# One layer of a hybrid decoder on one core: probabilities times values as float32 products

## The chip, the core and the metric

The kernel runs on one of the eight cores of a Trainium2 chip. A core has five engines that run side by side and wait for each other by semaphores: TensorE (PE in the profile; its weight loads are listed apart as PEld), VectorE (DVE), ScalarE (ACT), GpSimd (POOL) and SyncE (SP), which here issues the DMAs. The metric is the device time of one execution in microseconds (us).

## What is computed

One step of a decoder layer for a prompt of 1024 tokens and for 8 x 8 sampled tokens: RMS norm, an input projection to queries, keys, values and a state-space input, dilated sliding-window attention with 8 heads of 64 beside a state-space group, an output projection, and a gated feed-forward part. The change lies in the prompt's attention. For each of three branches (window, dilation) the reference computes

```python
scores = einsum('brcqhe,brckhe->brchqk', qs, kk) * HEAD_DIM ** -0.5
scores = where(mask, scores, -inf)
m = max(scores); p = exp(scores - m); den = sum(p)
out = einsum('brchqk,brckhe->brcqhe', p / den, vv)
```

and mixes the branches by their log sums. The kernel folds the three branches into two parts (`part` 0: neighbouring tokens, `part` 1: every fourth token) with scaled probabilities P, so that the output is the sum of P times V over both parts.

## The kernel before

Most large products are done in three: each float32 operand is cut into a high part, rounded to the fast type float32r (fp32r), and a low part, the remainder (`split`, lines 63 to 65: ACT writes the high part, DVE the low). `mm3` (line 68) multiplies high by high, high by low and low by high. Products that are issued by `mm1` (line 74) take their operands as they are: fp32r tiles, or float32 tiles, which the state-space part, its gate and the sample's scores use.

The prompt's attention (`prompt_attn`, line 1048) walks through 8 heads of 7 groups each (`GR`), a group being up to four blocks of 128 keys by 128 queries. For head `h` and group `g`:
- `score` multiplies queries and keys on PE (tiles QS, KH and KL, the latter with 64 rows) into a bank `pmm`; DVE adds the mask and takes the maximum (line 1123), and ACT takes the exponential (`expo`, line 1133);
- `norm` scales P by the branch factor, mostly on POOL (line 1176);
- `turn` transposes the blocks on PE (line 79) into a bank `ptr`, and `split` cuts the transposed P into PT's high part (ACT, line 64) and low part (DVE, line 65);
- `value` multiplies them with V on PE (line 75). Its weights are the tile VS, which holds V's high part in columns 0 to 63 and its low part in 64 to 127; its moving operand is PT's high part and then its low part, 128 or 256 columns each. So the bank `ppo` collects V's high part times P in partitions 0 to 63 and V's low part times P in 64 to 127, and after the last group of a half of the tokens ACT copies the upper half to `tmp` (line 1240) and DVE adds the two into `mixA` (line 1242).

`vloads` (line 1084) loads V for a pair of heads into VR (one buffer for each part) and cuts it into VS for each head, with ACT (line 1097) and DVE (line 1098). `value` of a group comes 11 steps of the loop behind its `score`; `vloads` of a head comes in step 4 of its 7.

The attention is merged by weights with other streams: in the first of two stages with the state-space part (`ssm_main`, from some 320 us), in the second (from some 445 us) with its gate and the sample's values (`sample_values`, tiles PX, vs; product line 75, low parts line 826 on DVE or POOL). A scheduler then sets the order of instructions on every engine, and each engine takes its own in that order. There is one bank `ppo`.

Of the kernel before, what the change touches and what calls it, by code (L numbers as in the profile page):

```python
# [42 lines left out]
def raw(ap):  # L43
    return ap.bitcast(F32)


class K:
# [1000 lines left out]
    def prompt_attn(self, ap):  # L1048
        nc, I = self.nc, self.I
        V, G = nc.vector, nc.gpsimd  # L1050
# [8 lines left out]
        HD, VH, P, ST, FC, PT, VR, po = ({} for _ in range(8))  # L1059


        def blocks(g):
            a, part, tiles = GR[g]
            out = []
            for j in tiles:
                two = a or (part == 0 and j)
                out.append((j, (0, 1) if two else (1,)))
            return out

        def loads(h):  # L1070
# [10 lines left out]
            HD[h] = (QS, KH, KL)  # L1081
            ST[h] = ap.tile([128, 2, 2, 2, 8], F32, tag="ST", name="ST", bufs=2)

        def vloads(h):
            if h % 2 == 0:
                es = slice(64 * h, 64 * h + 128)
                for part in range(2):
                    v = VR[h // 2, part] = ap.tile([128, 2, 4, 128], F32, tag=f"VR{part}", name="VR", bufs=1)
                    if part:
                        for a in range(2):  # L1090
                            self.load(v[:, a], vo[512 * a:512 * a + 512, es].rearrange("(p c) e -> p c e", c=4))
                    else:
                        self.load(v.rearrange("p a i e -> p (a i) e"), vo[:, es].rearrange("(i p) e -> p i e", p=128))
# [86 lines left out]
        def turn(h, g):  # L1180
            a, part, tiles = GR[g]
            nb = sum(len(ks) for _, ks in blocks(g))
            pt = self.bank("tr")
            for b in range(nb):
                self.tr(pt[:, 128 * b:128 * b + 128], P[h, g][:, b])
            d = PT[h, g] = ap.tile([128, 2, 4, 128], F32R, tag="PT", name="PT", bufs=PTB)
            src = pt[:, 0:128 * nb].rearrange("p (b q) -> p b q", q=128)
            hi, lo = d[:, 0, :nb], d[:, 1, :nb]
            if part == 0:
                src = src.rearrange("p b (r c) -> p b c r", c=4)  # L1190
                hi, lo = (z.rearrange("p b (c r) -> p b c r", c=4) for z in (hi, lo))
            self.split(hi, lo, src)


        def value(h, g):
            a, part, tiles = GR[g]
            VS = VH[h]
            if g in (0, 3):
                po[h, a] = self.bank("po")
            p = po[h, a]  # L1200
            d = PT[h, g]
            todo = []
            if part == 0:
# [12 lines left out]
            ops = []  # L1216
            if part == 0:
                for kt, l in todo:
                    j0, b0 = l[0]
                    out = p[:, 128 * j0:128 * j0 + 128 * len(l)]  # L1220
                    if len(l) == 2:
                        st = l[1][1] - b0
                        rhs = lambda hl, b0=b0, st=st: d[:, hl, b0:b0 + st + 1:st]
                    else:
                        rhs = lambda hl, b0=b0: d[:, hl, b0]
                    ops.append((out, VS[:, 0, kt], rhs))
            else:
                b = 0
                for j, ks in blocks(g):
                    for k in ks:  # L1230
                        kt = 4 * (a - 1 + k) + j
                        out = p.rearrange("p (s c r) -> p c s r", s=4, c=4)[:, j]
                        ops.append((out, VS[:, 1, kt], lambda hl, b=b: d[:, hl, b].rearrange("p (s r) -> p s r", s=4)))
# [12 lines left out]
        yield 0  # L1246
# [1 line left out]
        for n in range(56 + 7 + 4):  # L1248
            h, g = divmod(n, 7)
# [726 lines left out]
```

## Time and profile before

| | before |
|---|---|
| median of 3 runs | 1586.97 us (1584.7 to 1587.9) |
| profiled execution | 1586.99 us, span 1585.2 us |
| PE busy | 1451.3 us, 92% of the span |
| DVE busy | 1156.9 us, 73% |
| ACT, POOL busy | 718.1 us, 890.2 us |
| chain that ended last | PE 58%, DVE 21%, DMA 8% |
| products of P and V on PE (`ppo`) | 369.7 to 647.2 us |

The span runs from the first instruction to the last. An engine's busy time counts the time in which it works on something; matmuls overlap each other, so a record's duration is longer than the distance to the next record, and what a product costs is read from the distance between starts. A row of a timeline merges like instructions that follow each other: its start, the time from there to the end of the last one, and the count. The chain is followed back from the last instruction to what released it, and so on. The granted clock is the share of PE's full clock that it was given in a stretch: 1.00 is 2.4 GHz and 0.50 is 1.2 GHz.

### The profile page before, as it was taken

The page shows a single profiled execution, that of the slowest core. Times are in us where ns is not written, and L with a number is a line of the kernel's source. Part 1 is how long each engine was busy: PE and PEld are TensorE (multiplying, and loading weights), DVE is VectorE, ACT ScalarE, POOL GpSimd, SP SyncE. Part 2 cuts the span into 40 slices and gives each one's busy share as a digit, 9 for nine tenths or more (in the row PEclk, how much of TensorE's full clock was granted, in tenths as well). Part 3 has the DMA queues.
Part 4 walks back from the last instruction along what each step waited for, and adds up shares of the span by engine and source line. Part 5 has one row for each costly group of instructions (what it writes and reads, how often), then busy time and mean ns, then how long its engine had stood idle before and what let it go on. Part 6 is the DMA issues. An engine that isn't in the chain of part 4 may idle for free.

```text
span 1585.2 us, 27784 instructions
## 1 busy us (share of the span) xinstructions
PE 1451.3 (92%) x9909; PEld 1348.1 (85%) x9909; DVE 1156.9 (73%) x2178; ACT 718.1 (45%) x1831; POOL 890.2 (56%) x807
## 2 busy tenths in 40 slices
PE   6988988889999999899869999999999989988896
PEld 5978978867777677789859999999999979977896
DVE  6895489858757777688898555555555597799685
ACT  6233434345476766764444323233333453454343
POOL 3069445337635465555678656555553395678672
PEclk9998988859669999799989999999999999999998
DMA  8438888697775762633314332223332473384654
GB/s 218 155 132 286 239 245 228 195 230 191 200 199 162 200 180 80 177 99 109 110 40 129 104 103 91 83 88 89 92 102 82 147 269 122 127 305 142 185 156 121
DMA packets 213464, 246.20 MB, mean 155 GB/s; under 512 B 26798, under 2 KB 164878, under 8 KB 213326
## 3 DMA queue, kind: packets, MB, share of 16 engines
q1 hardware_dynamic: 213326, 244.43, 52.4%
q8 instruction: 78, 1.28, 0.4%
q14 instruction: 60, 0.49, 0.1%
HBM read 184.43 MB, written 59.95 MB: 154 GB/s over the span
## 4 chain that ended last, share of the span: by engine, by line
PE 58%; DVE 21%; DMA 8%; issue 5%; POOL 3%; ACT 3%; SPq 1%; DVEq 0%; POOLq 0%; ACTq 0%
PE pmm L72 14%; PE pmm L70 14%; PE pmm L71 14%; PE psd L75 7%; PE pmm L75 4%; DVE ws L65 4%; PE ppo L75 2%; PE ptr L79 2%; DMA kk<-in_cache_attn_k_dram 2%; DVE hT L1545 1%; DVE hn L65 1%; DVE hs L65 1%; DVE kk L680 1%; DVE Sm L687 1%; DMA wr<-in_w_in_dram 1%
## 5 line engine op out<-in xcount | busy, mean ns | idle before, releaser
L70 PE MATMUL pmm<-hn,ws 128*128 128x272 f32 x1232 | 359.3, 292 | 9.3 <-DVE s L1699 6.4
L72 PE MATMUL pmm<-hn,ws 128*128 128x272 f32 x1232 | 358.2, 291 | 3.1 <-DVE ws L65 3.1
L71 PE MATMUL pmm<-hn,ws 128*128 128x272 f32 x1232 | 357.9, 291 | 2.5 <-DVE hn L65 2.5
L65 DVE TENSOR_TENSOR ws<-wr,ws 128x512 fp32r<-128x512 f32 (+2 forms) x240 | 258.1, 1084 | 35.4 <-ACT ws L64 34.7
L70 PEld LDWEIGHTS pmm<-hn,ws 128*128 128x128 f32 x1232 | 234.3, 190 | 10.2 <-issue 7.7
L71 PEld LDWEIGHTS pmm<-hn,ws 128*128 128x128 f32 x1232 | 234.6, 190 | 3.1 <-DVE hn L65 3.1
L72 PEld LDWEIGHTS pmm<-hn,ws 128*128 128x128 f32 x1232 | 234.0, 190 | 3.6 <-DVE ws L65 3.4
L64 ACT ACTIVATE ws<-wr 128x512 fp32r<-128x512 f32 (+2 forms) x240 | 152.2, 642 | 173.8 <-PE pmm L72 165.9
L65 DVE TENSOR_TENSOR ws<-st,ws 128x512 fp32r<-128x512 f32 (+1 forms) x136 | 132.2, 975 | 82.9 <-ACT ws L64 82.0
L64 ACT ACTIVATE ws<-st 128x512 fp32r<-128x512 f32 (+1 forms) x136 | 83.6, 616 | 134.4 <-PE pmm L72 98.5
L72 PE MATMUL pmm<-hs,ws 128*128 128x272 f32 x448 | 133.3, 298 | 8.6 <-DVE ws L65 7.9
L70 PE MATMUL pmm<-hs,ws 128*128 128x272 f32 x448 | 132.4, 296 | 4.6 <-DVE hid L1699 4.3
L71 PE MATMUL pmm<-hs,ws 128*128 128x272 f32 x448 | 132.0, 295 | 0.1
L1619 POOL TENSOR_TENSOR st<-wr 128x512 f32<-128x512 f32 x40 | 56.7, 1417 | 102.0 <-DVE ws L65 101.2
L1706 POOL TENSOR_TENSOR hid<-hid,s 128x272 f32<-128x272 f32 x88 | 82.0, 938 | 43.7 <-DVE hid L1699 43.7
L826 POOL TENSOR_TENSOR vs<-vr,vs 128x512 fp32r<-128x512 f32 x40 | 55.6, 1398 | 86.5 <-ACT vs L824 75.0
L1627 POOL TENSOR_TENSOR st<-wr,st 128x512 f32<-128x512 f32 x40 | 57.8, 1444 | 80.3 <-DVE ws L65 80.3
L679 POOL TENSOR_TENSOR kf<-kf,qb 128x1024 f32<-128x1024 f32 x24 | 61.5, 2570 | 67.6 <-DMA kf<-in_cache_attn_k_dram 54.4
L72 PEld LDWEIGHTS pmm<-hs,ws 128*128 128x128 f32 x448 | 85.9, 192 | 11.4 <-DVE ws L65 11.3
L70 PEld LDWEIGHTS pmm<-hs,ws 128*128 128x128 f32 x448 | 86.3, 193 | 5.2 <-issue 4.5
L71 PEld LDWEIGHTS pmm<-hs,ws 128*128 128x128 f32 x448 | 86.3, 193 | 0.3 <-DVE hs L65 0.3
L1123 DVE CUSTOM_DVE_ANT_0 P<-pmm,lnc 128x256 f32<-128x256 f32 (+1 forms) x128 | 47.6, 377 | 52.7 <-PE pmm L75 42.2
(438 smaller groups left out, 4193.8 us busy)
## 6 DMA issues: line engine op xcount, KB each, us to landing
vr<-in_cache_attn_v_dram SPq DMA_DIRECT2D x80, 256.0 KB
wr<-in_ffn_w_down_dram SPq DMA_DIRECT2D x32, 512.0 KB
hs<-dH SPq DMA_DIRECT2D x28, 544.0 KB
kf<-in_cache_attn_k_dram SPq DMA_DIRECT2D x48, 256.0 KB
wr<-in_ffn_w_gate_dram SPq DMA_DIRECT2D x24, 512.0 KB
wr<-in_ffn_w_up_dram SPq DMA_DIRECT2D x24, 512.0 KB
dH<-hid SPq DMA_DIRECT2D x22, 544.0 KB
wr<-in_w_in_dram SPq DMA_DIRECT2D x16, 512.0 KB
```

Source lines behind the costliest of these rows:

```text
L64: self.nc.scalar.activation(hi, src, AF.Copy)
L65: (eng or self.nc.vector).tensor_tensor(out=lo, in0=src, in1=raw(hi), op=OP.subtract)
L70: nc.tensor.matmul(out, lhsT=wh, rhs=xh, start=start, stop=False)
L71: nc.tensor.matmul(out, lhsT=wh, rhs=xl, start=False, stop=False)
L72: nc.tensor.matmul(out, lhsT=wl, rhs=xh, start=False, stop=stop)
L75: self.nc.tensor.matmul(out, lhsT=w, rhs=x, start=start, stop=stop)
L679: nc.gpsimd.tensor_tensor(out=kf[i], in0=kf[i], in1=qb[b][:, 0:1].to_broadcast((128, 2, 512)), op=OP.mult)
L826: eng.tensor_tensor(out=s[:, 1], in0=vr[i], in1=raw(s[:, 0]), op=OP.subtract)
L1123: V.tensor_tensor_reduce(out=P[h, g].rearrange("p b k -> p (b k)")[:, o:o + n], in0=s[:, o:o + n], in1=lnc[:, part, 256 - n:256], scale=-1 ...
L1619: G.tensor_tensor(out=s1, in0=a[:, :, 128:256], in1=b[:, :, 128:256], op=OP.add)
L1627: self.nc.gpsimd.tensor_tensor(out=s2, in0=b[:, :, 0:128], in1=s2, op=OP.subtract)
L1706: G.tensor_tensor(out=o, in0=o, in1=sb, op=OP.mult)
```

## The change

P and V are no longer cut. `turn` copies the transposed P as float32 with ACT alone; PT has half the size and four buffers for two. `vloads` only loads, into two buffers for each part, and VS, its ACT copies and its DVE subtractions are gone. `value` issues one float32 product where it issued two, with the head's 64 columns of VR as weights, so the bank's partitions 64 to 127 stay unused, and the last step is one DVE copy from the bank to `mixA`.

```diff
-PB, VB, VSB, KKB, PTB, TAB, TCB, HSB, UB, CSB, WSB, HB = 10, 6, 4, 2, 2, 3, 2, 3, 2, 3, 5, 5
+PB, VB, VSB, KKB, PTB, TAB, TCB, HSB, UB, CSB, WSB, HB = 10, 6, 4, 2, 4, 3, 2, 3, 2, 3, 5, 5
...
         def vloads(h):
...
-                    v = VR[h // 2, part] = ap.tile([128, 2, 4, 128], F32, tag=f"VR{part}", name="VR", bufs=1)
...
-            VS = ap.tile([128, 2, 8, 128], F32R, tag="VS", name="VS", bufs=2)
             for part in range(2):
-                vv = VR[h // 2, part].rearrange("p a i e -> p (a i) e")[:, :, 64 * (h % 2):64 * (h % 2) + 64]
-                nc.scalar.activation(VS[:, part, :, 0:64], vv, AF.Copy)
-                V.tensor_tensor(out=VS[:, part, :, 64:128], in0=vv, in1=raw(VS[:, part, :, 0:64]), op=OP.subtract)
-            VH[h] = VS
+                v = VR[h // 2, part] = ap.tile([128, 2, 4, 128], F32, tag=f"VR{part}", name="VR", bufs=2)
...
-            d = PT[h, g] = ap.tile([128, 2, 4, 128], F32R, tag="PT", name="PT", bufs=PTB)
+            PT[h, g] = ap.tile([128, 4, 128], F32, tag="PT", name="PT", bufs=PTB)
+            d = PT[h, g][:, :nb]
...
-            self.split(hi, lo, src)
+            nc.scalar.activation(d, src, AF.Copy)
...
-            VS = VH[h]
+            v = VR[h // 2, part].rearrange("p a i e -> p (a i) e")[:, :, 64 * (h % 2):64 * (h % 2) + 64]
...
-            p = po[h, a]
+            p = po[h, a][0:64]
...
             for x, (out, w, rhs) in enumerate(ops):
-                for hl in range(2):
-                    self.mm1(out, w, rhs(hl), first and x == 0 and hl == 0, last and x == len(ops) - 1 and hl == 1)
+                self.mm1(out, w, rhs, first and x == 0, last and x == len(ops) - 1)
             if last:
-                tmp = ap.tile([64, 512], F32, tag="tmp", name="tmp", bufs=1)
-                nc.scalar.activation(tmp, p[64:128], AF.Copy)
                 dst = self.mixA[64 * (h % 2):64 * (h % 2) + 64, h // 2, 512 * a:512 * a + 512]
-                V.tensor_tensor(dst.rearrange("p (s r c) -> p s c r", s=4, c=4), p[0:64].rearrange("p (s c r) -> p s c r", s=4, c=4),
-                                tmp.rearrange("p (s c r) -> p s c r", s=4, c=4), op=OP.add)
+                V.tensor_copy(dst.rearrange("p (s r c) -> p s c r", s=4, c=4), p.rearrange("p (s c r) -> p s c r", s=4, c=4))
```

The scheduler orders the lighter program anew, in the two stages with attention. On DVE, in the first stage ahead of the second `Z` pair of that stage (a step of the sample's softmax; L927 to L929, L938, L946 and L948 are the state-space part, L1123, L1140, L1150 and L1151 before and L1119, L1136, L1146 and L1147 now are the mask, maxima and sums of the attention), before (388.7 to 391.7 us of the trace):

```order
L65 TENSOR_TENSOR PT<-ptr,PT 128x512
L938 SCALAR_TENSOR_TENSOR tb<-P_64,ta 128x128 x2
L782 TENSOR_SCALAR S<-S,mx 128x384
L948 COPY hf<-HS 128x4
L927 TENSOR_TENSOR ta<-psd,CS 128x256
L928 TENSOR_TENSOR tb<-psd,CS 64x256
```

and, from that `Z` pair to the scan L938 behind it, before (394.2 to 398.6 us):

```order
L790 TENSOR_TENSOR Z<-S,sel 128x768
L792 TENSOR_TENSOR Z<-S,sel 128x384
L1242 TENSOR_TENSOR mixA<-ppo,tmp 64x4x4x32
L946 TENSOR_TENSOR HS<-ta,tcc 128x2x128
L1151 TENSOR_REDUCE ST<-w 128x2x8
L1123 ISA P,ST<-pmm,lnc 128x128
L1123 ISA ST 128x1
L938 SCALAR_TENSOR_TENSOR tb<-P_64,ta 128x128 x2
```

Ahead of the same `Z` pair, now:

```order
L938 SCALAR_TENSOR_TENSOR tb<-P_64,ta 128x128 x2
L782 TENSOR_SCALAR S<-S,mx 128x384
L1147 TENSOR_REDUCE ST<-w 128x2x8
L948 COPY hf<-HS 128x4
L790 TENSOR_TENSOR Z<-S,sel 128x768
L792 TENSOR_TENSOR Z<-S,sel 128x384
```

and from the output's step behind that `Z` pair to the next scan, now:

```order
L1235 COPY mixA<-ppo 64x4x4x32
L946 TENSOR_TENSOR HS<-ta,tcc 128x2x128
L1119 ISA P,ST<-pmm,lnc 128x128
L1119 ISA ST 128x1
L1147 TENSOR_REDUCE ST<-w 128x2x8
L927 TENSOR_TENSOR ta<-psd,CS 128x256
L928 TENSOR_TENSOR tb<-psd,CS 64x256
L929 TENSOR_TENSOR tb<-psd,CS 64x256
L938 SCALAR_TENSOR_TENSOR tb<-P_64,ta 128x128 x2
```

The low part of P ahead of the `Z` pair is gone, and the output's step, one copy now, stands nine rows behind the pair where it stood right behind it.

On PE at the end of the second stage (`ptr<-ident,P` are the turns, `ppo` the products; an fp32r row of two products is a row of one float32 product now), before:

```order
L79 MATMUL ptr<-ident,P 128x128 x8
L75 MATMUL ppo<-PT,VS 128x256 x2
L75 MATMUL ppo<-PT,VS 128x128 x4
L75 MATMUL ppo<-PT,VS 128x256 x2
L75 MATMUL ppo<-PT,VS 128x128 x4
L79 MATMUL ptr<-ident,P 128x128 x4
L75 MATMUL ppo<-PT,VS 128x4x32 x16
```

and now:

```order
L79 MATMUL ptr<-ident,P 128x128 x8
L75 MATMUL ppo<-PT,VR 64x256
L75 MATMUL ppo<-PT,VR 64x128 x2
L75 MATMUL ppo<-PT,VR 64x256
L75 MATMUL ppo<-PT,VR 64x128 x2
L79 MATMUL ptr<-ident,P 128x128 x4
L75 MATMUL ppo<-PT,VR 64x4x32 x8
```

The order of the tail is the same, with half the products in each row. Taken together, the products stand in 74 stretches on PE before and in 64 now.

## Rows read from the trace of the kernel before

**Rows 1.** The products of P and V, by tile: count, ns least/median/most, first and last start

```profile
L75 PE MATMUL ppo<-PT,VS x368: 220/276/580, 369.7 to 647.2; 128*128 128x128 f32 x152, 128*128 128x256 f32 x32
```

**Rows 2.** Table by stretches: length; PE, PEld, DVE, ACT, POOL busy (count); clock; DMA

```profile
340.00:400.00 60.00, 52.39 (x269) 43.00 (x269) 53.20 (x159) 28.33 (x98) 42.02 (x66) 0.81 0.84 211
...
445.00:632.00 187.00, 184.09 (x826) 135.18 (x827) 133.47 (x351) 129.86 (x331) 96.27 (x113) 0.92 0.63 167
```

**Rows 3.** PE in order of time, fp32r products: start, us, engine, line, operation, count

```profile
573.66 0.28 PE L75 MATMUL ppo<-PT,VS 128*128 128x256 f32 x1
573.78 0.28 PE L75 MATMUL pmm<-KH,QS 128*128 128x256 f32 x1
...
577.31 0.73 PE L75 MATMUL ppo<-PT,VS 128*128 128x256 f32 x4
577.88 0.60 PE L79 MATMUL ptr<-ident,P 128*128 128x128 f32 x4
...
593.29 1.11 PE L75 MATMUL ppo<-PT,VS 128*128 128x128 f32 x8
594.24 0.63 PE L79 MATMUL psd<-ident,Z 128*128 128x128 f32 x4
```

**Rows 4.** PE in order of time, float32 products: sample's scores (kt), gate (mixS)

```profile
200.54 0.37 PE L72 MATMUL ppo<-xT,ws 128*128 128x448 f32 x1
200.74 0.37 PE L70 MATMUL ppo<-xT,ws 128*128 128x448 f32 x1
201.04 1.09 PE L75 MATMUL psd<-kt,QB 128*64 128x128 f32 x8
201.97 0.58 PE L75 MATMUL psd<-KN,QB 128*64 128x8 f32 x8
...
565.61 2.32 PE L75 MATMUL psd<-mixS,w 128*128 128x320 f32 x8
567.53 0.87 PE L75 MATMUL psd<-vs,PX 128*128 128x512 f32 x2
```

**Rows 5.** Groups by line, 310 to 660 us: count, busy us, mean ns, idle before

```profile
L65 DVE TENSOR_TENSOR PT<-ptr,PT 128x512 fp32r<-128x512 f32 x48 | 32.9, 684 | 10.8 <-ACT PT L64 10.6
L1242 DVE TENSOR_TENSOR mixA<-ppo,tmp 64x512 f32<-64x512 f32 x16 | 17.3, 1082 | 3.2 <-ACT tmp L1240 3.1
L1098 DVE TENSOR_TENSOR VS<-VR,VS 128x512 fp32r<-128x512 f32 x16 | 12.9, 826 | 0.0
L1240 ACT ACTIVATE tmp<-ppo 64x512 f32<-64x512 f32 x16 | 9.5, 595 | 6.0 <-PE ppo L75 5.8
```

**Rows 6.** The chain of work that ended last, in order of time: start, us, what

```profile
351.65 1.88 DVE VS L1098 x2
...
387.07 0.69 DVE PT L65
...
438.64 1.04 ACT VS L1097 x2
...
561.72 1.20 DVE VS L1098 x2
...
636.54 0.57 DVE PT L65
...
638.99 0.70 DVE PT L65
...
645.77 0.70 DVE PT L65
```

**Rows 7.** PE in order of time around its gap at 395 us

```profile
395.16 0.38 PE L75 MATMUL pmm<-KL,QS 64*128 64x256 f32 x1
398.66 0.57 PE L75 MATMUL psd<-U,WI 128*128 128x136 f32 x1 [3.11 <-DVE tb L938]
```

**Rows 8.** Table by stretches, two stretches at half clock (columns as in rows 2)

```profile
397.20:403.80 6.60, 5.14 (x21) 4.93 (x22) 6.00 (x23) 1.90 (x8) 4.43 (x6) 0.50 1.09 306
411.00:431.00 20.00, 19.79 (x73) 16.01 (x73) 13.03 (x39) 8.33 (x24) 12.31 (x21) 0.50 0.65 157
```

More of the change, by code (lines that the diff above doesn't have):

```diff
@@ L1058, in prompt_attn @@
         GR = [(0, 0, (0, 1)), (0, 0, (2, 3)), (0, 1, (0, 1, 2, 3)), (1, 0, (0, 1)), (1, 0, (2, 3)), (1, 1, (0, 1)), (1, 1, (2, 3))]
-        HD, VH, P, ST, FC, PT, VR, po = ({} for _ in range(8))
+        HD, P, ST, FC, PT, VR, po = ({} for _ in range(7))
         def blocks(g):
@@ L1084, in vloads @@
         def vloads(h):
-            if h % 2 == 0:
-                es = slice(64 * h, 64 * h + 128)
-                for part in range(2):
-                    v = VR[h // 2, part] = ap.tile([128, 2, 4, 128], F32, tag=f"VR{part}", name="VR", bufs=1)
[L1089 to L1093, printed above, removed]
-            VS = ap.tile([128, 2, 8, 128], F32R, tag="VS", name="VS", bufs=2)
-            for part in range(2):
-                vv = VR[h // 2, part].rearrange("p a i e -> p (a i) e")[:, :, 64 * (h % 2):64 * (h % 2) + 64]
-                nc.scalar.activation(VS[:, part, :, 0:64], vv, AF.Copy)
-                V.tensor_tensor(out=VS[:, part, :, 64:128], in0=vv, in1=raw(VS[:, part, :, 0:64]), op=OP.subtract)
-            VH[h] = VS
+            if h % 2:
+                return
+            es = slice(64 * h, 64 * h + 128)
+            for part in range(2):
+                v = VR[h // 2, part] = ap.tile([128, 2, 4, 128], F32, tag=f"VR{part}", name="VR", bufs=2)
+                if part:
+                    for a in range(2):
+                        self.load(v[:, a], vo[512 * a:512 * a + 512, es].rearrange("(p c) e -> p c e", c=4))
+                else:
+                    self.load(v.rearrange("p a i e -> p (a i) e"), vo[:, es].rearrange("(i p) e -> p i e", p=128))
         def cols(x, a, part, j):
@@ L1185, in turn @@
                 self.tr(pt[:, 128 * b:128 * b + 128], P[h, g][:, b])
-            d = PT[h, g] = ap.tile([128, 2, 4, 128], F32R, tag="PT", name="PT", bufs=PTB)
+            PT[h, g] = ap.tile([128, 4, 128], F32, tag="PT", name="PT", bufs=PTB)
+            d = PT[h, g][:, :nb]
             src = pt[:, 0:128 * nb].rearrange("p (b q) -> p b q", q=128)
-            hi, lo = d[:, 0, :nb], d[:, 1, :nb]
             if part == 0:
                 src = src.rearrange("p b (r c) -> p b c r", c=4)
-                hi, lo = (z.rearrange("p b (c r) -> p b c r", c=4) for z in (hi, lo))
-            self.split(hi, lo, src)
+                d = d.rearrange("p b (c r) -> p b c r", c=4)
+            nc.scalar.activation(d, src, AF.Copy)
         def value(h, g):
             a, part, tiles = GR[g]
-            VS = VH[h]
+            v = VR[h // 2, part].rearrange("p a i e -> p (a i) e")[:, :, 64 * (h % 2):64 * (h % 2) + 64]
             if g in (0, 3):
                 po[h, a] = self.bank("po")
-            p = po[h, a]
+            p = po[h, a][0:64]
             d = PT[h, g]
@@ L1222, in value @@
                         st = l[1][1] - b0
-                        rhs = lambda hl, b0=b0, st=st: d[:, hl, b0:b0 + st + 1:st]
+                        rhs = d[:, b0:b0 + st + 1:st]
                     else:
-                        rhs = lambda hl, b0=b0: d[:, hl, b0]
-                    ops.append((out, VS[:, 0, kt], rhs))
+                        rhs = d[:, b0]
+                    ops.append((out, v[:, kt], rhs))
             else:
@@ L1232, in value @@
                         out = p.rearrange("p (s c r) -> p c s r", s=4, c=4)[:, j]
-                        ops.append((out, VS[:, 1, kt], lambda hl, b=b: d[:, hl, b].rearrange("p (s r) -> p s r", s=4)))
+                        ops.append((out, v[:, kt], d[:, b].rearrange("p (s r) -> p s r", s=4)))
                         b += 1
             for x, (out, w, rhs) in enumerate(ops):
-                for hl in range(2):
-                    self.mm1(out, w, rhs(hl), first and x == 0 and hl == 0, last and x == len(ops) - 1 and hl == 1)
+                self.mm1(out, w, rhs, first and x == 0, last and x == len(ops) - 1)
             if last:
-                tmp = ap.tile([64, 512], F32, tag="tmp", name="tmp", bufs=1)
-                nc.scalar.activation(tmp, p[64:128], AF.Copy)
                 dst = self.mixA[64 * (h % 2):64 * (h % 2) + 64, h // 2, 512 * a:512 * a + 512]
-                V.tensor_tensor(dst.rearrange("p (s r c) -> p s c r", s=4, c=4), p[0:64].rearrange("p (s c r) -> p s c r", s=4, c=4),
-                                tmp.rearrange("p (s c r) -> p s c r", s=4, c=4), op=OP.add)
+                V.tensor_copy(dst.rearrange("p (s r c) -> p s c r", s=4, c=4), p.rearrange("p (s c r) -> p s c r", s=4, c=4))
         loads(0)
```

## The prediction

> **What bounds the kernel now.** I read the table by stretches first, to see in which stage the change acts, then the order of TensorE (PE) in time there, then the chain of work that ended last, and last the groups by line. The products of probabilities and values run from 370 to 647 us [rows 1]; after that, the output projection and the feed-forward part take the other 940 us of the 1585.2 us span, and the change leaves their instructions as they are. So all that can happen lies in some 300 us, which are two stages. From 340 to 400 us the state-space part and the attention run together: VectorE (DVE) is busy 53.2 of 60 us and PE 52.4, with a granted clock of 0.81 of full speed, which is a mixture of its two levels, 1.2 and 2.4 GHz [rows 2]. DVE is the tightest engine there. From 445 to 632 us attention shares PE with the gate and the sample's values: PE is busy 184.1 of 187 us, DVE 133.5 [rows 2]. There PE's own stream is the bound. In the last 18 us (632 to 650) turns and products follow each other, and each product waits for a copy.
>
> **What the change adds on PE.** A value product was two records, one for the high and one for the low part of P, with 128 columns of weights (V's high and low part side by side). It is one float32 product now, which this chip runs as two records (the score product of the sample part stands four times in the code and eight times in the trace [rows 4]). So 368 records stay 368, and the question is what one costs. *128 columns of P* (304 records): before, eight take 0.95 us from the first's start to the next instruction's, 0.119 us each [rows 3]; float32 with 64 columns of weights and 128 moving columns takes 0.93 us for eight, 0.116 us each [rows 4]. I take no difference. *256 columns of P* (64 records): before, one took 0.12 us (573.66 to 573.78), and two with two 128-wide ones behind them took 0.57 us, so (0.57 - 2 x 0.119) / 2 = 0.17 us each [rows 3]. No row shows a float32 product of 256 columns; the nearest are those of 320, of which eight take 1.92 us to the next start and 2.32 us to the end of the last, 0.24 to 0.29 us each [rows 4], so 0.19 to 0.23 us for 256. The cost is between 0.19 - 0.17 = 0.02 and 0.23 - 0.12 = 0.11 us a record, 1.3 to 7.0 us in all. I take 0.21 - 0.17 = 0.04 us, since the 0.17 comes from a stretch that is like most others: **+2.6 us** on the path.
>
> **What it removes.** On DVE the low parts of P go, 32.9 us in 48 instructions (8 smaller ones are not counted here), and those of V, 12.9 us in 16. The sum of two halves (16 of 1.08 us) becomes a copy of one [rows 5]; a copy of this pattern stands in no row, and its bounds are the 0.595 us of ScalarE's (ACT's) copy of the same 64x512 and the 1.08 us of the sum. Between them I take 0.8 us, so some 4.5 us. On ACT the 16 copies of a half go, 9.5 us [rows 5], and 16 copies of V's high part. That is about 50 us of DVE and 19 us of ACT, but most of it lies beside PE work and is worth nothing by itself. What counts is what the chain holds [rows 6]. Ahead of 632 us it holds V's parts with 1.88, 1.04 and 1.20 us and a low part of P with 0.69 us: 4.8 us. Behind each stands other work that is nearly as late (in the busy stretch DVE's own scans and evacuations), so I take three fifths, **-2.9 us**. In the tail each turn went PE, ACT, DVE, PE, and goes PE, ACT, PE now: three low parts of 0.57, 0.70 and 0.70 us are on the chain, and two half copies of 0.6 us [rows 5] stood ahead of the sums there: 3.2 us. ACT's squares are close behind there, so I take two thirds, **-2.2 us**.
>
> **A gap that the busy DVE makes.** PE ends its work at 395.2 us and starts again at 398.66 us, released by DVE's scan [rows 7]. DVE had worked without a gap; in its row ahead of that scan stand two low parts of P and a sum (the order in the section on the change shows one of them and the sum), 2 x 0.68 + 1.08 us. After that gap the granted clock is 0.50 from 397.2 to 403.8 us, and PE is busy 5.1 us of it [rows 8], of which half, 2.6 us, is the slow clock. Of the 3.1 us of idle time and these 2.6 us I take back **-2.5 us**; the bounds are 0 and 5.7.
>
> **The sum** is +2.6 - 2.9 - 2.2 - 2.5 = -5.0 us. The profiled execution took 1586.99 us (span 1585.2 and 1.8 around it), and the median of the runs is 1586.97, so the two can be set equal: 1587 - 5 = **1582 us**.
>
> Edits without a price: P's copy on ACT keeps its shape and only its output type changes. PT with four buffers of half the size holds what it held, and V with two buffers no longer waits for a split ahead of a reload. The products now read V straight from its load, but the first does so 7 steps after that load is issued, where a split stood before; if that cover were gone, PE would wait for the load, as ACT did. The scheduler moves instructions between the stages' streams, as the order shows, and I give that no sign.
>
> **Rivals.**
> *Slower: PE's stream pays in full, and the freed DVE is idle.* One mechanism, at the border of the value products on PE. Ahead of float32 products with 64 columns of weights the step from the last fp32r one took 0.30 us (200.74 to 201.04) where those ahead of it are 0.20 us apart [rows 4], as if the first weight load lay open. With 64 stretches of value products in the new order, that is 64 x 0.09 = 5.8 us, and with the high end of the 256-wide records 7.0 us: +12.8. If the PE-bound stage gives nothing back and only the tail does, it is 12.8 - 2.2 = +10.6, 1598 us; it decides from where PE's additions pass the 7.6 us returned. Against it: 29 of these stretches begin behind a score product with 64 rows, where the load lies open before as well. I give it 0.19, mostly at a part of that price (around 1592).
>
> *Much slower: the array's passes count.* A single-pass record of 448 columns takes 0.20 us [rows 4], so 128 columns are 0.058 us of array time. Two single-pass records are 0.116 us of it; the two float32 records take 0.23 us together, as four passes would. If the old pair cost what its array time is, the new one costs +0.116 x 152 products of 128 and twice that x 32 of 256: 25 us, so 1612 us. Against it stand the equal 0.119 and 0.116 us a record: the old records took twice their array time, since something else paced them. 0.04. The Trainium skill says so in "FP8 and Floating Point Precision", section "TensorE Precision Notes": true float32 is four passes through the array. By it alone the two passes of the old pair would double; the trace agrees on the passes of the new form, and differs on what the old one cost.
>
> *Nothing to be measured: cover.* The work that is removed had another wait just behind it; POOL (scaling of P and the state-space part) is busy 42.0 of 60 us in the DVE-bound stretch [rows 2], and it and the loads set the pace. Then -2 for the tail and +2.6 for PE, 1587.5 us. 0.20.
>
> *Much faster: the clock.* From 411 to 431 us the granted clock is 0.50 too, with 19.8 us of PE work [rows 8]. If the lighter DVE lets PE run on through this stage, half of it, 9.9 us, comes back besides: 1572 us. No row shows that DVE alone causes that stretch. 0.17.
>
> **How the numbers follow.** A measurement of this kernel can tell 0.2%, 3.2 us, from no change: faster is below 1583.8, slower above 1590.1. The forecast has 0.40 (0.32 of it below 1583.8, 0.08 above), cover 0.20, the clock 0.17, the PE rival 0.19 (0.02 of it within the bound), the passes 0.04. Faster is 0.32 + 0.17 = 0.49, the same 0.08 + 0.20 + 0.02 = 0.30, slower 0.17 + 0.04 = 0.21. The range reaches from 1571 (the clock rival) to 1592 (the common part of the PE rival); left out are the passes, the dearer half of the PE rival and a little below the clock's: 0.18.
>
> **What would show it.** Right: 368 value records, the 256-wide ones near 0.21 us apart and the 128-wide ones near 0.115; DVE some 9 us less busy from 340 to 400 us and the gap at 395 us shorter; the tail from the last sample product to the last output of attention 2 us shorter. Wrong: a gap of 0.09 us or more ahead of most value stretches; the clock at 0.50 in more of the 320 to 445 us stretch than now; PE waiting for V's load; or the stages before 310 us or behind 760 us changed, where no instruction differs but by chance of order.

## The result and the profile after

The changed kernel took 1597.09 us (median of five runs, 1593.65 to 1598.74) where the kernel before took 1586.97: a ratio of 1.0068 with a 95% interval of 1.004 to 1.0096, so slower by 0.7%, or 10 us. On a second chip, beside the experiments, the ratio was 1.0015 (0.9989 to 1.0041). Slower or no change, then, and not the gain that was forecast. The kernel before took 1591.1, 1589.3 and 1591.1 us in the three jobs of timed experiments below, so ratios are compared from job to job, not times.

The profiled execution has a span of 1595.3 us against 1585.2. First the table by stretches, which answers to [rows 2]:

```profile
340.00:400.00 60.00, 55.30 (x259) 44.15 (x259) 43.82 (x138) 24.09 (x85) 36.26 (x59) 0.74 0.82 193
...
445.00:632.00 187.00, 185.79 (x797) 125.31 (x797) 107.47 (x301) 118.57 (x308) 81.96 (x103) 0.95 0.62 163
```

DVE (third busy time) is relieved as forecast: 43.8 us for 53.2, and 107.5 for 133.5. PE (first) is not: 185.8 of 187 us for 184.1, and that at a higher granted clock, 0.95 for 0.92. The same 187 us held 797 records where they had held 826. So PE takes longer for a record, in the mean.

Where the time went shows in three lengths. From the start to the first score product: 322.0 us (320.2 before). From there to the end of the last product of P and V, which is called *the attention* below: 334.7 us (327.3). From there to the end: 938.6 us (937.7). Of the 10.1 us, 7.4 lie in the attention. The other parts hold the same instructions; in the three traces of the kernel before that there are by now the first part took 320.2, 323.2 and 316.9 us, so a difference of 2 us there lies within that spread.

The products by tile, as in [rows 1]:

```profile
L75 PE MATMUL ppo<-PT,VR x368: 272/273/689, 375.7 to 656.4; 128*64 128x128 f32 x152, 128*64 128x256 f32 x32
```

They are 368 records again. PE in order of time around two stretches of them, as in [rows 3] (start, duration, form, count):

```profile
574.78 0.71 PE L75 MATMUL psd<-vs,PX 128*128 128x512 f32 x2
575.49 0.86 PE L75 MATMUL ppo<-PT,VR 128*64 128x256 f32 x4
576.29 0.66 PE L79 MATMUL ptr<-ident,P 128*128 128x128 f32 x4
...
582.11 0.39 PE L75 MATMUL pmm<-KH,QS 128*128 128x256 f32 x1
582.43 0.38 PE L75 MATMUL pmm<-KL,QS 64*128 64x256 f32 x1
582.74 0.65 PE L75 MATMUL ppo<-PT,VR 128*64 128x128 f32 x4
...
594.05 0.32 PE L75 MATMUL pmm<-KL,QS 64*128 64x128 f32 x1
594.30 0.43 PE L75 MATMUL ppo<-PT,VR 128*64 128x128 f32 x2
594.66 0.33 PE L79 MATMUL psd<-ident,Z 128*128 128x128 f32 x1
```

A row of four (two of 256 columns, two of 128) took 0.80 us to the next start (575.49 to 576.29); the like row of before took 0.57 (577.31 to 577.88 in [rows 3]). A row of two took 0.36 us (594.30 to 594.66), and inside a stretch a record of 128 columns takes only 0.109 us. The rest lies behind the last record of a stretch.

The groups by line, 310 to 660 us, as in [rows 5]:

```profile
L1188 ACT ACTIVATE PT<-ptr 128x512 f32<-128x512 f32 (+1 forms) x56 | 31.5, 577 | 23.6 <-PE ptr L79 23.4
L1235 DVE COPY mixA<-ppo 64x512 f32<-64x512 f32 x16 | 17.3, 1080 | 14.9 <-PE ppo L75 14.3
```

The copy into `mixA` costs 1.080 us, as the sum did (1.082 in [rows 5]). And the chain, as in [rows 6]:

```profile
401.81 0.99 DVE mixA L1235
...
598.57 1.07 DVE mixA L1235
...
640.95 1.02 DVE rb L844
642.20 0.73 DVE f L1161
643.02 0.84 POOL P L1172 x2
649.01 0.61 ACT PT L1188
```

V's parts and P's low parts have left it. The copy into `mixA` is on it twice, and the ACT copy of P four times, all in the last 8 us of the attention.

### The profile page after: what moved, and what is told of

Read it like the earlier page. It is cut to its first block, busy times and chain, and to the rows that moved or that the text cites. A ratio compares the mean times of both kernels' runs of the same rounds, so it can differ in the third digit from the quotient of the medians.

```text
span 1595.3 us, 27646 instructions
## 1 busy us (share of the span) xinstructions
PE 1461.4 (92%) x9909; PEld 1339.8 (84%) x9909; DVE 1126.7 (71%) x2106; ACT 702.6 (44%) x1799; POOL 885.2 (55%) x807
## 4 chain that ended last, share of the span: by engine, by line
PE 63%; DVE 19%; DMA 8%; issue 4%; POOL 3%; ACT 2%; SPq 1%; DVEq 0%; POOLq 0%; ACTq 0%
PE pmm L72 14%; PE pmm L70 13%; PE pmm L71 13%; PE psd L75 8%; PE pmm L75 5%; DVE ws L65 4%; PE ppo L75 3%; PE ptr L79 3%; DVE hT L1537 1%; DVE hn L65 1%; DVE hs L65 1%; DMA kk<-in_cache_attn_k_dram 1%; DMA hs<-dH 1%; POOL acc L1409 1%; DMA out_dram<-yf 1%
## 5 line engine op out<-in xcount | busy, mean ns | idle before, releaser
L826 POOL TENSOR_TENSOR vs<-vr,vs 128x512 fp32r<-128x512 f32 x40 | 52.3, 1312 | 95.9 <-ACT vs L824 94.6
L1119 DVE CUSTOM_DVE_ANT_0 P<-pmm,lnc 128x256 f32<-128x256 f32 (+1 forms) x128 | 48.1, 379 | 78.0 <-PE pmm L75 72.4
L72 PEld LDWEIGHTS pmm<-hs,ws 128*128 128x128 f32 x448 | 87.1, 195 | 11.0 <-DVE ws L65 10.0
L70 PEld LDWEIGHTS pmm<-hs,ws 128*128 128x128 f32 x448 | 87.4, 195 | 6.1 <-issue 5.0
L71 PEld LDWEIGHTS pmm<-hs,ws 128*128 128x128 f32 x448 | 87.5, 195 | 0.6 <-DVE hs L65 0.6
```

What stands on the lines that cost most here:

```text
L70: nc.tensor.matmul(out, lhsT=wh, rhs=xh, start=start, stop=False)
L71: nc.tensor.matmul(out, lhsT=wh, rhs=xl, start=False, stop=False)
L72: nc.tensor.matmul(out, lhsT=wl, rhs=xh, start=False, stop=stop)
L826: eng.tensor_tensor(out=s[:, 1], in0=vr[i], in1=raw(s[:, 0]), op=OP.subtract)
L1119: V.tensor_tensor_reduce(out=P[h, g].rearrange("p b k -> p (b k)")[:, o:o + n], in0=s[:, o:o + n], in1=lnc[:, part, 256 - n:256], scale=-1 ...
```

## What a step of PE costs: an account of the attention

For each kernel below, the distance from each product's start to the next one's was taken from the trace between the first score product and the last product of P and V, counted half where the granted clock is 0.50 (which is what is called full-clock time below), with the waits (no record running) taken out. Only steps that begin or end with a product of P and V are in the first five columns. "Narrow" is 64 columns of weights, "wide" 128. All in us, each rounded by itself; the last two columns are the length of the attention and how much of it ran at half clock.

| kernel | inside a stretch | leaving it | entering from a 64-row score product | entering from another | sum | attention | half clock |
|---|---|---|---|---|---|---|---|
| before (fp32r pairs, wide) | 35.5 | 9.7 | 9.3 | 8.2 | 62.7 | 327.3 | 97 |
| changed (float32, narrow) | 43.2 | 13.2 | 10.7 | 9.8 | 76.7 | 334.7 | 76 |
| float32, wide | 44.7 | 4.8 | 12.1 | 4.6 | 66.2 | 323.2 | 79 |
| float32, narrow for four heads | 43.5 | 8.2 | 9.2 | 8.2 | 69.1 | 330.3 | 80 |
| fp32r pairs, wide, changed DVE work | 35.5 | 7.3 | 9.2 | 6.9 | 59.0 | 321.4 | 95 |
| fp32r pairs, narrow | 24.0 | 7.3 | 10.8 | 6.2 | 48.3 | 315.8 | 91 |
| three fp32r products, narrow | 36.2 | 7.7 | 11.9 | 8.0 | 63.9 | 316.7 | 73 |

Second traces of three of them repeat the sum within 0.2 us (before twice more, changed, and float32 wide once more), while the half clock moves by 10 us. So the change costs PE 76.7 - 62.7 = 14.0 us at full clock; 7.7 of it lie inside the stretches and 6.4 at their borders. That split holds the new order too. There are 64 stretches where there were 74, and of the 64 records of 256 columns 62 have another product of their stretch behind them where 48 had. These 14 steps, at the 0.176 us that such a step took before, move 2.5 us from the borders to the inside. By form, then, some 5 us belong to the inside and some 9 to the borders.

## The experiments

The theory after the result was the slower rival of the prediction, in a sharper form: float32 products with 64 columns of weights cost PE time at both borders of a stretch. The rivals were that float32 as such costs it, and that the scheduler's new order does.

**128 columns of weights.** V's tile holds two heads side by side, so all 128 columns can be the weights, and the copy takes the half of the bank that belongs to the head.

```diff
-            v = VR[h // 2, part].rearrange("p a i e -> p (a i) e")[:, :, 64 * (h % 2):64 * (h % 2) + 64]
+            v = VR[h // 2, part].rearrange("p a i e -> p (a i) e")
-            p = po[h, a][0:64]
+            p = po[h, a]
...
             if last:
+                p = p[64 * (h % 2):64 * (h % 2) + 64]
```

> The changed kernel with all 128 columns of V's tile (both heads of the pair) as weights; the copy takes the half that belongs to the head. The product stays float32, with as many records and the same work on the other engines. Theory 'border': a stretch of value products with 64 columns of weights pays when PE enters it and when it leaves it: 62 exits at 0.203 us where 0.112 stood before, 14 entries at 0.33 for 0.23 us and 22 at 0.20 for 0.03 us, some 11 us in all. With 128 columns that goes: 1586 us. Rival 'stream': float32 itself costs more than the pair of fp32r products did (256 columns above all): still 1597 us. Rival 'order': the scheduler's new order costs the time: also 1597 us, if the order stays much as it is.

Measured: 0.9933 of before (0.9911 to 0.9955). PE in order of time:

```profile
569.85 0.92 PE L75 MATMUL ppo<-PT,VR 128*128 128x256 f32 x4
570.61 0.60 PE L79 MATMUL ptr<-ident,P 128*128 128x128 f32 x4
...
584.44 0.38 PE L75 MATMUL ppo<-PT,VR 128*128 128x128 f32 x2
584.58 0.36 PE L75 MATMUL pmm<-KH,QS 128*128 128x256 f32 x1
```

Two wide products and the step out of them take 0.14 us, where two narrow ones took 0.36. Medians of the steps at full clock say the same: out of a narrow float32 stretch 0.203 us behind a record of 128 columns, whatever follows; out of a wide one 0.112 into a float32 product and 0.031 into an fp32r one; into a narrow one 0.20 behind turns and the like and 0.327 behind the sample's values, into a wide one 0.11 and 0.233. The exits (64, and 60 in the wide kernel) make 8.3 us of the table's difference and the entries 3.7; inside, the wide form costs 1.5 more. Net 76.7 - 66.2 = 10.5 us, and the attention is 334.7 - 323.2 = 11.5 us shorter. Both were then run on one chip:

> The changed kernel itself, beside the next three on one chip, so that they can be compared with it directly. 1.0068 of the kernel before, as it was measured; the variant with 128 columns of V is then 0.7% to 1.4% faster than it. Theory 'border': 11 us (0.7%) by the steps between records at full clock; more than 17 us (1.1%) would need something besides.

> The variant with 128 columns of V's tile as weights once more, on the chip of the changed kernel's second run. 0.993 of the kernel before as measured, and 11 us (theory 'border') to 21 us (as the ratios so far would have it) less than the changed kernel.

Measured: the changed kernel 1.0015 (0.9989 to 1.0041), the wide one 0.9902 (0.987 to 0.9934); medians 1591.1 and 1577.1 us, 14 us apart; attention 331.2 and 320.6 us, 10.6 apart. In full-clock time without the waits, all of PE's steps in the attention take 286.1 and 287.9 us in the two traces of the changed kernel and 273.3 and 274.6 us in those of the wide one. So the border accounts for 10.5 of some 13 us on PE; the rest, and some 3 us between the medians and the attention's length, stay open.

**Half of the heads narrow.**

```diff
+            wd = 64 + 64 * (h % 2)
-            v = VR[h // 2, part].rearrange("p a i e -> p (a i) e")[:, :, 64 * (h % 2):64 * (h % 2) + 64]
+            v = VR[h // 2, part].rearrange("p a i e -> p (a i) e")[:, :, 0:wd]
-            p = po[h, a][0:64]
+            p = po[h, a][0:wd]
...
             if last:
+                p = p[64 * (h % 2):64 * (h % 2) + 64]
```

> The changed kernel with 64 columns of V as weights for the four even heads and 128 columns for the four odd ones; all else is the changed kernel's. Theory 'border': the price is by stretch, so about half of it remains, and attention (first score product to last product of P and V), which took 334.7 and 331.2 us with 64 columns and 323.2 and 320.6 with 128, takes 327 to 328 us; total about half way, 0.997 of before. Rival 'order' (the two schedules differ by luck): attention's time lies near one of the ends, 321 to 323 or 331 to 335 us.

Measured: 1.0007 (0.998 to 1.0034). On PE's account the kernel lies between the two: 8.2 us for leaving, where narrow has 13.2 and wide 4.8; the sum is 69.1 between 66.2 and 76.7. The length is not half way: 330.3 us of attention, near the changed kernel's 331.2 and 334.7. It ran 80 us of it at half clock, the others 66 to 79. In full-clock time without the waits all of PE's steps take 279.5 us, about half way between the 273.3 and 274.6 of wide and the 286.1 and 287.9 of narrow. So PE's steps bear the border theory out, the time alone does not.

**Narrow, but in fp32r.** The kernel before with 64 columns of weights; V's low part times P is left out.

```diff
-            p = po[h, a]
+            p = po[h, a][0:64]
-                    ops.append((out, VS[:, 0, kt], rhs))
+                    ops.append((out, VS[:, 0, kt, 0:64], rhs))
...
-                nc.scalar.activation(tmp, p[64:128], AF.Copy)
+                nc.scalar.activation(tmp, p, AF.Copy)
```

> The kernel before with 64 columns of weights: only V's high part is multiplied (V's low part times P is left out), and the last step copies and adds the same 64 rows twice, so ACT, DVE and the number of products stay. Theory 'border': a change of the number of weight columns costs the same for fp32r: 74 stretches with some 0.09 us at the exit and 0.1 us or more at the entry where no 64-row product is ahead: +8 to +13 us, 1595 to 1600 us. Rival 'float32 alone has it': 1587 us. Should a 64-column weight load be shorter, so that fp32r products of 128 columns come closer than 0.112 us, up to 304 x 0.05 = 15 us come back against it.

Measured: 0.9938 (0.9909 to 0.9966), a miss for the theory as it stood. PE in order of time:

```profile
580.71 0.50 PE L75 MATMUL psd<-vs,PX 128*128 128x512 f32 x1
581.05 0.58 PE L75 MATMUL ppo<-PT,VS 128*64 128x128 f32 x7
581.46 1.06 PE L79 MATMUL ptr<-ident,P 128*128 128x128 f32 x8
```

Seven products take 0.41 us to the next start, 0.059 each, the step out of them included, where fp32r with 128 columns of weights took 0.119 [rows 3]. So a narrow stretch in fp32r has no border price, and the price belongs to float32 and 64 columns together. And the step of the fp32r pair of before halves with the weight columns. The load of its weights is the nearest cause, but that it sets the pace is argued and not shown: the load's own record goes from 0.192 to 0.136 us.

**The relief without the price.** DVE's work of the changed kernel with the product stream of before: P's high part alone, used in both products; the low parts of P and V are left out.

```diff
+                vr = VR[h // 2, part] = ap.tile([128, 2, 4, 128], F32R, tag=f"VS{part}", name="VS", bufs=2)
+                nc.scalar.activation(vr, v, AF.Copy)
...
-            PT[h, g] = ap.tile([128, 4, 128], F32, tag="PT", name="PT", bufs=PTB)
+            PT[h, g] = ap.tile([128, 4, 128], F32R, tag="PT", name="PT", bufs=PTB)
...
-                self.mm1(out, w, rhs, first and x == 0, last and x == len(ops) - 1)
+                for hl in range(2):
+                    self.mm1(out, w, rhs, first and x == 0 and hl == 0, last and x == len(ops) - 1 and hl == 1)
```

> The changed kernel with the product stream of before: P as fp32r high part alone, used in both products of a pair (the low parts of P and of V are left out, so the attention comes out doubled), weights of 128 columns in fp32r, made by 8 ACT copies of a pair of heads. DVE has the changed kernel's work, PE the records of the kernel before. Theory 'border': this is the relief without the price on PE; the relief was priced at 7.6 us, the price of 256-wide float32 products falls away too: 1580 us. Rival 'cover' (the work taken from DVE and ACT lay beside other work): 1587 us, as the kernel before. Rival 'order' : some 1595 us.

Measured: 0.9921 (0.9894 to 0.9948), 0.8% or some 12 us less than before. The relief is worth something, and in time more than the 7.6 us that the prediction gave it. Part of that is the clock and the order: in full-clock time the attention of this kernel's two traces is 273.9 and 276.1 us, 2.5 to 6.3 less than the 278.6 to 280.2 of before, and 3.4 to 3.8 of it are at the products, which stand in 61 stretches for 74. Whether the relief lies in DVE's load was asked next.

**DVE's load put back.** The wide float32 kernel, with the 56 subtractions into a tile that nothing reads.

```diff
             nc.scalar.activation(d, src, AF.Copy)
+            lo = ap.tile([128, 4, 128], F32, tag="LO", name="LO", bufs=2)[:, :nb]
...
+            V.tensor_tensor(out=lo, in0=src, in1=d, op=OP.subtract)
```

> The variant with 128 columns of V, with the 56 subtractions of P's low part put back on DVE, into a tile that nothing reads. PE's products are those of that variant, and no product waits for DVE. If DVE's load itself sets the pace where it is full (340 to 400 us), some 3 to 6 us slower than that variant (0.996 of before). If only the wait of the products for the low part counted (the chain), as that variant (0.993).

Measured: 0.9896 (0.9868 to 0.9923), no slower than without them (0.9902 on the same chip). PE's waits in the attention are 12.6 and 14.5 us in two traces, and 14.3 and 14.1 without the subtractions, so DVE's load makes PE wait no longer here. The time alone would not show it, since the order moved as well (52 stretches for 60) and the half clock fell to 51 and 56 us from 79 and 69: in full-clock time the attention is 288.3 and 287.3 us, and was 283.8 and 286.0.

**The clock.** The wide float32 kernel has 3.5 us more than before at the products of P and V in full-clock time (66.2 for 62.7), and an attention that is 4.1 us shorter. It ran fewer microseconds at half clock. Four more traces were taken for that.

> A second trace of the kernel before, for the clock in the attention (first score product to last product of P and V). In the first, 97 us of those 327 ran at half clock; the kernels with float32 products of P and V had 51 to 80 us. If the float32 stream returns clock time, this trace has 90 us and more again; if it is chance, 60 to 80 us, and then a shorter attention than 327 us.

> A third trace of the kernel before, for the same question: 90 us and more at half clock if it belongs to the kernel, 60 to 80 us if it is chance.

> A second trace of the variant with the fp32r pairs of before (high part of P alone, used twice; the low parts of P and V are left out) and the changed kernel's work on DVE. The first had 95 us at half clock and an attention of 321.4 us. If the float32 stream returns clock time, 90 us and more again; if DVE's relief does or if it is chance, fewer.

> A second trace of the variant with 128 columns of V in float32 and P's low part put back on DVE. The first had 51 us at half clock and an attention of 313.6 us. If the float32 stream returns clock time, 50 to 80 us again, whatever DVE does; if it is chance, up to 97.

Measured, at half clock in the attention: before 93 and 103 us (97 in the first trace), fp32r pairs with the changed DVE work 70 (95), float32 with DVE's load put back 56 (51). The row of the attention in the table by stretches, for one trace each of three kernels (columns as in [rows 2]: length, busy times of PE, PEld, DVE, ACT and POOL, clock, DMA):

```profile
323.20:650.10 326.90, 310.62 (x1447) 237.22 (x1448) 241.53 (x673) 203.51 (x557) 178.65 (x250) 0.86 0.69 178
```

```profile
317.10:628.40 311.30, 300.69 (x1443) 232.09 (x1443) 200.07 (x601) 193.91 (x532) 169.03 (x248) 0.89 0.71 185
```

```profile
320.70:635.80 315.10, 300.61 (x1446) 232.02 (x1447) 230.15 (x657) 186.23 (x526) 171.39 (x250) 0.91 0.71 183
```

The first is the kernel before, the second the fp32r pairs, the third float32 with DVE's load. The last has the highest clock with DVE at 230 us of work, so DVE's load alone doesn't take the clock away. The three traces of before lie at 93 to 103 us, the eight of float32 kernels with 64-row scores (two each of changed, wide and load put back, one each of four narrow heads and of the buffers below) at 51 to 80, so the difference between before and these is hardly chance. But float32 doesn't explain it alone, since fp32r pairs with the changed DVE work lie at 95 and 70 and the three narrow fp32r products below at 73. Nor does the shorter path from a turn to its product: the pairs have it, the three narrow products don't. The cause stays open.

**Buffers.**

```diff
-PB, VB, VSB, KKB, PTB, TAB, TCB, HSB, UB, CSB, WSB, HB = 10, 6, 4, 2, 4, 3, 2, 3, 2, 3, 5, 5
+PB, VB, VSB, KKB, PTB, TAB, TCB, HSB, UB, CSB, WSB, HB = 10, 6, 4, 2, 2, 3, 2, 3, 2, 3, 5, 5
...
-                v = VR[h // 2, part] = ap.tile([128, 2, 4, 128], F32, tag=f"VR{part}", name="VR", bufs=2)
+                v = VR[h // 2, part] = ap.tile([128, 2, 4, 128], F32, tag=f"VR{part}", name="VR", bufs=1)
```

> The variant with 128 columns of V, with two buffers for the transposed P and one for each part of V, as many as the kernel before has. If the buffers were without effect, as the prediction has it: 0.990 to 0.993 of before. If they carry the relief: slower by 3 us and more, up to 1585 us, with waits of turns for PT or of V's load for the last product of its pair.

Measured: 0.9954 (0.9929 to 0.9979), a time that the second forecast has. Its mechanism isn't there: the attention took 319.4 us, no longer than the 320.6 and 323.2 with more buffers, and PE's waits in it 13.9 us for 14.1 and 14.3. The part ahead of it took 328.6 us, 9 to 10 more than theirs; at its end PE waits 10.5 us for a load of K, and 5.2 and 5.3 in theirs. This traced execution was the slowest of its twelve, 7.5 us over their median. So the buffers don't carry the relief in the attention; whether they cost the part ahead of it anything, which the scheduler also orders anew, isn't settled.

**Three narrow fp32r products** (V high by P high, V high by P low, V low by P high; V low by P low, which the wide pair held, is left out), into the same 64 rows.

```diff
-                for hl in range(2):
-                    self.mm1(out, w, rhs(hl), first and x == 0 and hl == 0, last and x == len(ops) - 1 and hl == 1)
+                for k, (wl, hl) in enumerate(((0, 0), (0, 1), (1, 0))):
+                    self.mm1(out, w[:, 64 * wl:64 * wl + 64], rhs(hl), first and x == 0 and k == 0, last and x == len(ops) - 1 and k == 2)
...
-                nc.scalar.activation(tmp, p[64:128], AF.Copy)
...
+                V.tensor_copy(dst.rearrange("p (s r c) -> p s c r", s=4, c=4), p.rearrange("p (s c r) -> p s c r", s=4, c=4))
```

> The kernel before with three fp32r products of 64 columns (V high by P high, V high by P low, V low by P high) in the place of two with 128, all into the same 64 rows, so that the half copy on ACT goes and the sum on DVE becomes a copy; P and V are still cut on ACT and DVE. At the steps that the run with 64 columns of fp32r showed (0.060 us for 128 moving columns, 0.118 for 256) 128 columns cost 0.18 us where they cost 0.224, and 256 cost 0.35 where they cost 0.34: 152 x 0.044 = 6.7 us less on PE, and 2 to 4 us less from the shorter end. Theory 'weight load' (an fp32r product of 128 columns is paced by the load of its 128 weight columns): 0.994 of before, 1577 us. Rival 'order or clock' (the run with 64 columns was faster for another reason): as before, 1587 us.

Measured: 0.9887 (0.9853 to 0.9921). The steps are those expected (0.060 us for 128 columns), and yet the account's sum is 63.9 us, not below the 62.7 of before: 184 records more and more borders (83 stretches for 74) take back what each saves. The attention is 10 us shorter all the same, with 73 us at half clock. The forecast of the time held; its working did not.

**128 rows for the scores.** The dearest steps of the attention are those at the score products with 64 rows: ahead of the 128 of them and behind them lie 84.7 us at full clock in the kernel before. K's low part was loaded twice, one below the other, so that these products have 128 rows too (with Q's low part times K's low part added), in the wide float32 kernel and in the one with three narrow products.

```diff
-            KL = ap.tile([64, 1024], F32R, tag="KL", name="KL", bufs=2)
+            KL = ap.tile([128, 1024], F32R, tag="KL", name="KL", bufs=2)
...
-            self.load(raw(KL), raw(self.dK[1, hs]))
+                self.load(raw(KL[64 * l:64 * l + 64]), raw(self.dK[1, hs]))
...
-                self.mm1(s[:, o:o + n], qs[0:64], keys(KL, a, part, j, two), False, True)
+                self.mm1(s[:, o:o + n], qs, keys(KL, a, part, j, two), False, True)
```

> As the kernel with 128 columns of V, and the score products with the low part of K also made with 128 rows instead of 64 (the low part of K loaded twice, one below the other, so that the low part of Q times the low part of K is added). If a change of the number of rows lays the weight load open as one of the columns does, the 128 products with 64 rows (0.31 to 0.53 us to the next start, and 0.32 to 0.39 ahead of them, where fp32r products of 256 columns and 128 rows are 0.12 to 0.17 apart) lose some 0.1 to 0.2 us on each side: 25 to 45 us less on PE, of which DVE and the loads may keep a half: 1550 to 1570 us. If rows cost nothing, 1586 us or what the kernel with 128 columns of V shows.

> Three fp32r products of 64 columns, P and V cut as in the kernel before, and the score products with the low part of K made with 128 rows. Three narrow products alone gave 0.989 of before; the 128 rows gave 0.989 where 128 columns of V alone gave 0.993 and 0.990, some 5 us. If the two add up: 0.985 of before, 1566 us. Rival 'another engine is the bound by then' (DVE with both low parts and the loads): 0.989, 1572 us.

Measured: 0.9888 (0.9856 to 0.992) and 0.9892 (0.9851 to 0.9933). PE in order of time, wide float32 with 128 rows:

```profile
566.25 0.28 PE L75 MATMUL pmm<-KH,QS 128*128 128x256 f32 x1
566.37 0.28 PE L75 MATMUL pmm<-KL,QS 128*128 128x256 f32 x1
566.49 0.81 PE L75 MATMUL ppo<-PT,VR 128*128 128x256 f32 x4
```

The steps ahead of the product and behind it are 0.12 us each; with 64 rows they were 0.32 and 0.31 (582.11 to 582.74 in the changed kernel above). Ahead of these products and behind them lie 56.0 us, where the wide kernel with 64 rows has 88.0. The attention is 309.5 and 306.2 us long, but PE's waits in it grew from 14 us in either kernel with 64 rows to 42 and 40, so little of the gain is left: by then PE waits for others (in the wide kernel 14.0 us for the maxima on DVE, line 1119, where it was 5.4), and the two changes don't add up. The first forecast, 1550 to 1570 us, was too fast; of the second's two the rival's came (0.989). The wide kernel with 128 rows is 1.1% faster than before and 1.8% than the changed kernel (by its first ratio), with V and P uncut; the narrow one with 64 rows is as fast (0.9887).

## Why the prediction was wrong, by its steps

The forecast was -5.0 us; +10 (or +2, on the second chip) was measured. The slower rival came nearest: it named the borders, and its 12.8 us of PE time are close to the 14.0 of the account. It put the border's price at the entries alone, though; against before the exits took 3.5 us more and the entries 2.9. It was given 0.19.

- *128 columns of P: no difference.* Right inside a stretch, 0.109 us a record for 0.112.
- *256 columns: 0.21 us against 0.17, +2.6.* Too low, but within its bounds of 1.3 to 7.0. They took 0.216 us into a record of 128 columns and 0.26 (mean) into one of 256, 0.24 a record, against a mean of 0.176 in the kernel before: 0.06 x 64 is some 4 us. The +7.7 inside the stretches also hold 1.4 us at records of 128 columns and the 14 steps that the new order put there.
- *The borders.* This is the step that failed: they had no term in the sum. The row that priced them as a rival showed the entry (200.74 to 201.04 in [rows 4]) and was read. The exit stands in the same trace and was not: the eight products at 201.97 in [rows 4] have 64 columns of weights and 8 moving ones and follow each other at 0.054 us in the mean, and the step out of the last, to the row below, is 0.133 us. In the changed kernel each of 64 stretches pays 0.203 us or more at its exit, and entries behind turns take 0.20 us where they took 0.03, those behind the sample's values 0.33 for 0.23. Both borders together took 6.4 us more than before, with ten stretches fewer, and 12.0 more than with 128 columns of weights.

```profile
202.48 0.66 PE L79 MATMUL psd<-ident,kn 128*128 128x128 f32 x4
```

- *The chain, -2.9, and the gap at 395 us, -2.5.* PE's waits in the attention were 15.3, 16.3 and 17.2 us in the traces of before and are 13.5 and 13.4: some 2 to 4 us came back, from all causes. DVE's load was the wrong cause, since putting it back made PE wait no longer. In the first stage another wait stands now, on a load (PE, the widest gap between 380 and 415 us):

```profile
406.40 0.50 PE L75 MATMUL pmm<-KH,QS 128*128 128x128 f32 x1 [2.02 <-DMA U<-dU]
```

- *The copy into mixA at 0.8 us.* Wrong, 1.08. One operand fewer saved nothing, and the 4.5 us of it are not there. The pattern of the output is the same in both; that it sets the time was not tried.
- *The tail, -2.2* (two thirds of its 3.2 us are 2.1, not 2.2). From the last eight turns of a group of 256-column products to the last product it got shorter, 5.93 us for 6.78, as the low parts left. But ahead of it PE waits now:

```profile
642.35 0.41 PE L75 MATMUL psd<-csel,rb 128*128 128x64 f32 x2 [2.22 <-DVE rb L845]
643.45 2.05 PE L79 MATMUL ptr<-ident,P 128*128 128x128 f32 x7 [0.69 <-POOL P L1172]
...
650.67 1.09 PE L79 MATMUL ptr<-ident,P 128*128 128x128 f32 x8
...
656.60 0.65 PE L75 MATMUL ptr<-ones,acc 128*68 128x1 f32 x8
```

The last turns stand behind the sample's sum (`rb`), and the scale of their P behind it on DVE (640.95 to 643.02 us in the chain above). From the last of the sample's values to the last product of P and V it is 16.5 us for 13.5. The new order did that, and the prediction gave the order no sign.
- *The clock.* In the sum it stood as the 2.6 us behind the gap at 395 us, taken together with the gap at less than half; a rival had 9.9 us, for which DVE was named. Half-clock time fell from 93 to 103 us to 76 and 66, which returns some 8 to 18 us, in the changed kernel too. Without it the loss would be larger. Its cause isn't DVE's load alone, and stays open.

In full-clock time the attention grew by 16 to 20 us (296.5 and 298.2 against 278.6 to 280.2): 14.0 at the value products, less 2 to 3 of PE's waits, which are counted at full clock here. The other 5 to 7 lie in the rest of PE's stream, in another order: 2.5 at the sample's values, of which nine more have no product of P and V beside them, some 2 on the way from a score product to the one with 64 rows, and the rest was not followed further.

## What to carry over

Price a new form of product at three places: inside a stretch of its like, at the step into it and at the step out of it; a trace that has the form anywhere shows all three. Where half of the array would idle anyway, try a float32 product with all 128 columns of weights and an fp32r product with all 128 rows, with whatever lies beside the operand: the 1.5 us that the columns cost inside were paid back at the borders, and the rows took their steps from 0.32 to 0.12 us. This is no rule for every form, since fp32r products with 64 columns were the cheaper ones. And work taken from an engine that is busy but not waited for is worth little by itself: with the same subtractions put back off the path, PE waited no longer.

## What the runs showed of the hardware that was not expected

- Float32 products with 64 weight columns: 0.203 us at the exit (behind 128 moving columns), whatever follows; with 128 columns 0.112 into float32 and 0.031 into fp32r. Fp32r with 64 columns has no such step (0.060).
- Fp32r products of 128 moving columns follow at 0.112 us with 128 weight columns and at 0.060 with 64.
- Fp32r products with 64 rows among products with 128: 0.32 and 0.31 us around one of 256 columns, against 0.12 and 0.12 with 128 rows.
- Float32 of 256 moving columns (0.216 to 0.267 us a record) is no cheaper than two of 128 (0.109 each).
- The granted clock of the attention moved from kernel to kernel and between traces of one: 93 to 103 us at half clock in three traces of the kernel before, 51 to 80 in eight of the float32 kernels, 95 and 70 in two of the fp32r pairs with the changed DVE work. The cause was not found.
